# One hybrid decoder layer on one core: a written-out TensorE order for the norm stage, with two feed-forward products placed around the last tile's transposes

## The chip, the cores and the metric

The kernel runs on one core of one Trainium2 chip. The metric is the device time of one execution in microseconds (us), as the median of several runs; lower is better. A profile of one execution stands beside it.

## The reference

One layer of a decoder trunk, on 1024 tokens of width 1024, all in float32. Only the second half of the layer is touched by the change:

```python
mixed = jnp.concatenate([out_a..., out_b...], axis=-1)     # outputs of the two attention groups
x = x + ga1 * (mixed @ w_out[l])                           # 1024 -> 1024
h2 = rmsnorm(x, g_ffn[l]) * (1.0 + sc2) + sh2
gate, up = jnp.split(h2 @ w_gu[l], 2, axis=-1)             # 1024 -> 2 x 2816
x = x + ga2 * ((jax.nn.silu(gate) * up) @ w_down[l])
return rmsnorm(x, g_final)
```

## The kernel before

The tokens lie in eight tiles of 128. Every float32 matrix product is made of three products of rounded parts (low by high, high by high, high by low), so each operand is split into a high part (a copy on ScalarE) and a low part (a subtraction on VectorE or GpSimd). The feed-forward products are further combined in Winograd's manner: the activations and the weights are quartered, and sums of quarters are multiplied.

The stage in question begins once attention is done. A first pass multiplies all tiles by the first half of w_out (lines 1126 to 1137). The second pass, called the norm stage here, runs over the tiles in the order 0, 4, 1, 5, 2, 6, 3, 7 (line 1099), in the loop of lines 1217 to 1222. For a tile, `normed` loads the second half of the mixed rows, splits them (line 1108 on ScalarE, line 1109 on GpSimd), makes 24 products with w_out (two column halves of 12, through `mm3`, lines 366 to 368), adds them to the residual (line 1173, VectorE), sums the squares (line 1176, ScalarE), stores the residual to DRAM from the GpSimd queue (line 1177), computes the reciprocal root in small steps (`rstd_parts`, lines 157 to 163) and writes the normalized rows into `xn` (line 1179, VectorE). There is one `xn`, so a tile's rows can be written only when its predecessor's have been transposed. `turned` transposes `xn` in eight blocks on TensorE (line 1186), four into a PSUM bank of the kind `tp`, four into one of the kind `o`, and brings them back with scale and shift (line 1190 on ScalarE, line 1193 on VectorE). `combined` forms the quarter sums and splits them (lines 1159 and 1160, and sums at 1202 and 1208 to 1214): a tile below 4 completes columns of the quarters `22` and `S1`; a tile from 4 on completes columns of `11`, `S3`, `S2`, `12` and `S4`, and needs its partner of the lower half. The last tile below 4 is tile 3, the seventh in order; the last of all is tile 7.

The feed-forward loop (line 1291) then takes 22 blocks of 128 columns of w_gu. For each, `ff_prep` loads four weight quarters over the SP queue into the buffers that the residual tiles held (`ff_w`, line 1247), makes sums of them (`t1` to `t4`), and splits seven operands (`page_split`, lines 1240 on ScalarE and 1241 on VectorE); `ff_mm` makes a product of 12 matmuls (lines 1256 to 1258). In the first block the product of `w1` with `S1` (called p5) and that of `w4` with `22` (called p4) are written ahead of the other five, of which the first is `w11` with the quarter `11`.

What sets the order: each engine works through its own queue in order. A scheduler orders the queues ahead of time from the order of the program, from priorities and from its estimate of when inputs are ready. It may therefore place products of later tiles ahead of a tile's transposes. `ahead(PF)` (lines 1225, 1251 and 1292) raises the priority of the first block's preparation by 100. `on_pe` (line 759) takes that freedom away for the TensorE instructions that go through it: each is queued behind the one before it. Before the change the attention uses it and the norm stage doesn't.

Of the kernel before, what the change touches and what calls it, by code (L numbers as in the profile page):

```python
# [19 lines left out]
D = 1024  # L20
S = 1024
P = 128
# [46 lines left out]
def hybrid_block(ctx, tc, x, c, w_ada, b_ada, g_attn, w_in, kv_norm_g, w_uk, w_uv, w_out, g_ffn,  # L69
                 w_gu, w_down, g_final, lnm, out, dbg=None):  # L70
    nc = tc.nc
    V, A, G, PE = nc.vector, nc.scalar, nc.gpsimd, nc.tensor
# [23 lines left out]
    def mm_tile(tag="mm"):  # L96
        return ps["pool"].tile([P, 512], F32, name=tag, tag=tag, bufs=ps[tag])
# [24 lines left out]
    ident = const.tile([P, P], F32, name="ident")  # L122
# [31 lines left out]
    def rstd_parts(ss, width):  # L154

        m = small.tile([P, 8], F32, name="rm", tag="rm")[:, :1]
        V.tensor_scalar(m, ss, 1.0 / width, EPS, op0=OP.mult, op1=OP.add)
        y = small.tile([P, 8], F32, name="ry", tag="ry")[:, :1]
        A.activation(y, m, AF.Sqrt)
        V.reciprocal(y, y)  # L160
        t = small.tile([P, 8], F32, name="rt", tag="rt")[:, :1]
        V.scalar_tensor_tensor(t, y, m, y, op0=OP.mult, op1=OP.mult)
        V.tensor_scalar(t, t, -0.5, 1.5, op0=OP.mult, op1=OP.add)
        return y, t
# [193 lines left out]

    mods = modulation()

    def mm3(p, lhs, rhs, ks):

        n = len(ks)
        for j, k in enumerate(ks):
            (ah, al), (bh, bl) = lhs(k), rhs(k)
            PE.matmul(p, al, bh, start=(j == 0), stop=False)  # L366
            PE.matmul(p, ah, bh, start=False, stop=False)  # L367
            PE.matmul(p, ah, bl, start=False, stop=(j == n - 1))  # L368

    def pair3(ps_, qh, ql, qs, kh, kl_, ks, mm=PE.matmul):  # L370

# [302 lines left out]
    while True:  # L674
        while made < due:
            with behind(signed[0]):
                ev, n = next(work)
# [81 lines left out]
    def on_pe(op, *args, **kw):  # L759

        with tc.issue_after(pe_last[0].ins) if pe_last[0] else nullcontext():
            pe_last[0] = op(*args, **kw)  # L762
# [266 lines left out]
    for t in range(NT):  # L1029
        p = mm_tile()  # L1030
# [63 lines left out]
    f6 = [wk.tile([P, 3, 512], F32, name=f"f6{i}") for i in range(2)]  # L1094
# [4 lines left out]
    order = [0, 4, 1, 5, 2, 6, 3, 7]  # L1099
# [3 lines left out]
    def mixed(g, t):  # L1103
# [5 lines left out]
        (G if g else V).tensor_tensor(ml, mr, mh.bitcast(F32), op=OP.subtract)  # L1109
        return mh, ml  # L1110

    def w_out_part(m, w, e):
        p = mm_tile()
        cs = slice(e * 512, e * 512 + 512)
        mm3(p, lambda k: (m[0][:, k], m[1][:, k]), lambda k: (w[0][:, k, cs], w[1][:, k, cs]), range(4))
        return p

    first = order[4:] + order[:4]
# [8 lines left out]
    for i, t in enumerate(first):  # L1127
        m = mixed(0, t)
        residual(i + 1)
        for e in range(2):  # L1130
            cs = slice(e * 512, e * 512 + 512)
# [11 lines left out]
    def quarters(at, names):  # L1143
        return {n: [at.tile([P, 4, 512], F32R, name=f"A{n}{x}") for x in "hl"] for n in names}

    qA = quarters(pool(qr_ctx, "qR"), ("11", "S2"))
    qA.update(quarters(pool(qa_ctx, "qS"), ("S1", "22", "12", "S3", "S4")))
    xn = f6[0][:, 0:2].rearrange("p a b -> p (a b)")
# [4 lines left out]
    def h32_tile():  # L1153
        nh32[0] += 1
        return h32s[(nh32[0] - 1) % len(h32s)]
# [6 lines left out]
    R2, R1, EV = "GVG", "VGGVVVGG", "AAVAAAVA"  # L1162
    hq = {}

    def normed(n, t):

        if n >= 4:
            acc[t] = slot[n - 4]
            nc.sync.dma_start(acc[t], spill_y[n - 4])
        m = mixed(1, t)  # L1170
        for e in range(2):
            cs = slice(e * 512, e * 512 + 512)
            V.tensor_tensor(acc[t][:, cs], acc[t][:, cs], w_out_part(m, wo1, e), op=OP.add)
        dump(("x1", t), acc[t])
        ss = small.tile([P, 8], F32, name="ss", tag="ss")[:, :1]
        A.activation(f2.bitcast(BF), acc[t], AF.Square, accum_out=ss)
        G.dma_start(spill_x[t], acc[t])
        y, u = rstd_parts(ss, D)
        V.tensor_scalar(xn, acc[t], u, y, op0=OP.mult, op1=OP.mult)

    def turned(t):
        hq[t] = [h32_tile().rearrange("p (a b) -> p a b", b=P) for _ in range(2)]
        for k0, hv in zip((0, 4), hq[t]):
            p = mm_tile(("tp", "o")[k0 // 4])
            for k in range(4):
                PE.transpose(p[:, k * P:(k + 1) * P], xn[:, (k0 + k) * P:(k0 + k + 1) * P], ident)
            for k in range(4):
                kk = k0 + k
                if EV[kk] == "A":
                    A.activation(hv[:, k], p[:, k * P:(k + 1) * P], AF.Identity,  # L1190
                                 scale=a2[:, kk:kk + 1], bias=s2[:, kk:kk + 1])
                else:
                    V.tensor_scalar(hv[:, k], p[:, k * P:(k + 1) * P], a2[:, kk:kk + 1], s2[:, kk:kk + 1],
                                    op0=OP.mult, op1=OP.add)

    def combined(t):

        sl = slice(t % 4 * P, t % 4 * P + P)
        ha, hb = hq[t]
        if t < 4:  # L1200
            e_ = [{'G': G, 'V': V}[x] for x in R2]
            e_[0].tensor_tensor(s_, ha, hb, op=OP.add)
            split("22", hb, sl, e_[1])
            split("S1", s_, sl, e_[2])
            return
        a21, a22 = hq[t - 4]
        e_ = [{'G': G, 'V': V}[x] for x in R1]
        e_[0].tensor_tensor(a21, ha, a21, op=OP.subtract)
        e_[1].tensor_tensor(a22, a22, a21, op=OP.subtract)
        split("11", ha, sl, e_[3])  # L1210
        split("S3", a21, sl, e_[4])
        split("S2", a22, sl, e_[5])
        split("12", hb, sl, e_[6])
        e_[2].tensor_tensor(hb, hb, a22, op=OP.subtract)
        split("S4", hb, sl, e_[7])

    for n, t in enumerate(order):
        normed(n, t)
        turned(t)
        if n:  # L1220
            combined(order[n - 1])
    combined(order[-1])


    PF, PD = 100, 50
# [11 lines left out]
    def page_split(src):  # L1237
        h_, l_ = (pages[(used[0] + i) % len(pages)] for i in range(2))
        used[0] += 2
        A.activation(h_, src, AF.Copy)  # L1240
        V.tensor_tensor(l_, src, h_.bitcast(F32), op=OP.subtract)  # L1241
        return h_, l_
# [7 lines left out]
    def ahead(n):  # L1250
        return tc.high_priority(n) if n else nullcontext()

    def ff_mm(w, a, tag):
        p = mm_tile(tag)
        for k in range(4):
            PE.matmul(p, w[1][:, k], a[0][:, k], start=(k == 0), stop=False)  # L1256
            PE.matmul(p, w[0][:, k], a[0][:, k], start=False, stop=False)  # L1257
            PE.matmul(p, w[0][:, k], a[1][:, k], start=False, stop=(k == 3))  # L1258
        return p

    def u_tile():
# [3 lines left out]
    def ff_prep(f):  # L1265
        b11, b21 = ff_w(f * P)
        b12, b22 = ff_w(DFF + f * P)
        t1, t2, t3, t4 = tsum
        if f == 0:
            V.tensor_tensor(t1, b12, b11, op=OP.subtract)  # L1270
            w1 = page_split(t1)
            V.tensor_tensor(t2, b22, t1, op=OP.subtract)
            G.tensor_tensor(t4, b21, t2, op=OP.subtract)
            w4 = page_split(t4)
            w11 = page_split(b11)
        else:
            w11 = page_split(b11)
            G.tensor_tensor(t1, b12, b11, op=OP.subtract)
            G.tensor_tensor(t2, b22, t1, op=OP.subtract)
        w2 = page_split(t2)  # L1280
        w21 = page_split(b21)
        G.tensor_tensor(t3, b22, b12, op=OP.subtract)
        w3 = page_split(t3)
        if f > 0:
            w1 = page_split(t1)
            G.tensor_tensor(t4, b21, t2, op=OP.subtract)
            w4 = page_split(t4)
        w22 = page_split(b22)
        return w11, w21, w1, w2, w3, w4, w22

    for f in range(NF):
        with ahead(PF if f == 0 else 0):
            w11, w21, w1, w2, w3, w4, w22 = ff_prep(f)
        x_, u2, u3, u5 = [u_tile() for _ in range(4)]
        if f == 0:
            p5, p4 = ff_mm(w1, qA["S1"], "tp"), ff_mm(w4, qA["22"], "o")
        A.activation(x_, ff_mm(w11, qA["11"], "mm"), AF.Copy)
        V.tensor_tensor(u2, ff_mm(w2, qA["S2"], "tp"), x_, op=OP.add)
        V.tensor_tensor(x_, ff_mm(w21, qA["12"], "mm"), x_, op=OP.add)
        A.activation(x_, x_, AF.Silu)  # L1300
        V.tensor_tensor(u3, ff_mm(w3, qA["S3"], "mm"), u2, op=OP.add)
        if f > 0:
            p5 = ff_mm(w1, qA["S1"], "tp")
        V.tensor_tensor(u5, p5, u3, op=OP.add)
        V.tensor_tensor(u2, p5, u2, op=OP.add)
        if f > 0:
            p4 = ff_mm(w4, qA["22"], "o")
        V.tensor_tensor(u3, p4, u3, op=OP.add)
        A.activation(u3, u3, AF.Silu)  # L1309
        G.tensor_tensor(u5, u3, u5, op=OP.mult)  # L1310
        G.dma_start(spill_g[f][:, :512], u5)
        V.tensor_tensor(u2, ff_mm(w22, qA["S4"], "mm"), u2, op=OP.add)
        G.tensor_tensor(u2, x_, u2, op=OP.mult)
        G.dma_start(spill_g[f][:, 512:], u2)
# [230 lines left out]
```

## Time and profile before

| what | value |
|---|---|
| median of 3 runs | 1441.33 us (1437.42 to 1443.82) |
| the profiled execution's own time | 1437.92 us |
| its span, from the first to the last instruction | 1436.1 us |
| mean granted TensorE clock | 0.961 |
| TensorE busy | 1297.0 us (90%) |
| VectorE busy | 1016.3 us (71%) |
| GpSimd busy | 674.9 us (47%) |
| ScalarE busy | 598.8 us (42%) |

The norm stage lies at about 664 to 740 us of the span; the loop of the feed-forward part follows up to about 1166 us. A row of a timeline has the start, the duration, the engine, the line and the operation with its operands; "x4" says that four were merged into the row; in brackets stands how long the engine had been idle before, and what ended that. Names in a row are those of buffers: `f` stands for several buffers of the working pool (`xn`, the residual tiles, the sums), `wo` for the w_out buffers that later hold weight splits, `AS1l` for the low part of the quarter sum S1. PE is TensorE, DVE VectorE, ACT ScalarE, POOL GpSimd, SP the queue that issues most loads.

### The profile page before, as it was taken

How to read it: one execution, taken by the hardware profiler on the slowest of the kernel's cores; microseconds unless marked ns; L12 is line 12 of the kernel's file. 1: busy time of each engine (PE TensorE's matmuls, PEld its weight loads, DVE VectorE, ACT ScalarE, POOL GpSimd, SP SyncE). 2: the span in 40 equal slices, each digit the busy share in tenths (PEclk: the TensorE clock that was granted, in tenths of full speed). 3: DMA queues.
4: the chain of work that ended last, by engine and by line, in shares of the span. 5: the costliest groups of instructions: out<-in, count | busy, mean ns of one | idle time of the engine just before them, and what ended most of it. 6: DMA issues, size and time to landing. Idle time of an engine off the chain costs nothing.

```text
span 1436.1 us, 20358 instructions
## 1 busy us (share of the span) xinstructions
PE 1297.0 (90%) x7477; PEld 1033.9 (72%) x7477; DVE 1016.3 (71%) x1754; ACT 598.8 (42%) x1217; POOL 674.9 (47%) x454
## 2 busy tenths in 40 slices
PE   2999898999878899999869999999999998888894
PEld 0566776798666677787748888888888886766773
DVE  4136899999887477644987545554545569999997
ACT  3435546461456565613763333333333223223334
POOL 1650311324330598122676444445544436487865
PEclk9999898999989999999979999999999999999997
DMA  9723124233311444273423222222223281404004
GB/s 240 238 75 117 30 67 125 91 101 95 126 52 54 147 142 119 76 227 114 161 79 98 89 88 81 66 88 81 81 88 96 87 322 46 154 23 154 0 1 118
DMA packets 133018, 152.11 MB, mean 106 GB/s; under 512 B 9715, under 2 KB 95540, under 8 KB 132918
## 3 DMA queue, kind: packets, MB, share of 16 engines
q1 hardware_dynamic: 122160, 129.56, 29.8%
q0 software_dynamic: 4672, 15.73, 2.9%
q10 hardware_dynamic: 6086, 5.52, 1.5%
q8 instruction: 59, 0.97, 0.3%
q14 instruction: 41, 0.34, 0.1%
HBM read 115.65 MB, written 34.60 MB: 105 GB/s over the span
## 4 chain that ended last, share of the span: by engine, by line
PE 49%; DVE 29%; POOL 8%; DMA 6%; issue 5%; ACT 3%; SPq 1%; DVEq 0%; ACTq 0%; POOLq 0%
DVE score L620 7%; PE mm L1258 6%; PE mm L1256 6%; PE mm L1257 6%; PE tp L1256 3%; PE tp L1258 3%; PE tp L1257 3%; PE mm L366 3%; PE mm L368 3%; PE mm L367 2%; PE o L762 2%; DVE yacc L1376 2%; PE mm L762 2%; PE tp L762 2%; DVE score L424 2%
## 5 line engine op out<-in xcount | busy, mean ns | idle before, releaser
L1240 ACT ACTIVATE wo<-f 128x512 fp32r<-128x512 f32 x124 | 78.0, 631 | 178.0 <-PE mm L1258 78.8
L1241 DVE TENSOR_TENSOR wo<-f,wo 128x512 fp32r<-128x512 f32 x124 | 102.7, 831 | 43.8 <-ACT wo L1240 41.9
L366 PE MATMUL mm<-hh,wl 128*128 128x512 f32 (+2 forms) x288 | 111.7, 389 | 0.0
L367 PE MATMUL mm<-hh,wh 128*128 128x512 f32 (+2 forms) x288 | 111.2, 387 | 0.0
L368 PE MATMUL mm<-hl,wh 128*128 128x512 f32 (+2 forms) x288 | 108.1, 385 | 0.0
L214 POOL TENSOR_SCALAR wh<-wraw 128x1024 fp32r<-128x1024 f32 (+1 forms) x20 | 20.3, 1032 | 132.6 <-PE mm L368 82.3
L366 PE MATMUL mm<-wo,wo 128*128 128x512 f32 x148 | 59.0, 398 | 10.1 <-DVE wo L1366 10.1
L215 POOL TENSOR_TENSOR wl<-wraw,wh 128x1024 fp32r<-128x1024 f32 (+1 forms) x22 | 52.6, 2410 | 29.8 <-ACT ry L144 29.7
L366 PEld LDWEIGHTS mm<-hh,wl 128*128 128x128 f32 (+1 forms) x288 | 54.4, 189 | 15.2 <-issue 2.8
L368 PEld LDWEIGHTS mm<-hl,wh 128*128 128x128 f32 (+1 forms) x288 | 53.7, 188 | 14.0 <-issue 2.2
L367 PEld LDWEIGHTS mm<-hh,wh 128*128 128x128 f32 (+1 forms) x288 | 54.6, 190 | 11.5 <-issue 1.1
L368 PE MATMUL mm<-wo,wo 128*128 128x512 f32 x148 | 56.9, 393 | 1.7 <-DVE wo L1366 1.7
L367 PE MATMUL mm<-wo,wo 128*128 128x512 f32 x148 | 58.2, 393 | 0.0
L793 ACT ACTIVATE ttB<-ttB,mn 128x128 f32<-128x128 f32 (+7 forms) x64 | 49.1, 768 | 15.5 <-DVE mn L789 14.9
L1366 DVE TENSOR_TENSOR wo<-f,wo 128x1536 fp32r<-128x1536 f32 (+1 forms) x17 | 55.1, 3246 | 0.0
L1310 POOL TENSOR_TENSOR f<-f 128x512 f32<-128x512 f32 x15 | 19.8, 1322 | 74.2 <-ACT f L1309 74.2
L366 PE MATMUL mm<-wo,ml 128*128 128x512 f32 x128 | 51.6, 403 | 1.8 <-DVE ml L1109 1.8
L762 PE MATMUL tp<-ident,ttB 128*128 128x128 f32 x288 | 43.6, 294 | 10.2 <-ACT ptB L808 9.7
L620 DVE TENSOR_SCALAR_CACHE_REDUCE score<-kl,sc 128x1024 bf16<-128x1024 uint16 (+2 forms) x48 | 52.3, 1140 | 0.0
L620 DVE TENSOR_SCALAR_CACHE_REDUCE score<-ka,sc 128x768 bf16<-128x768 int16 (+2 forms) x48 | 52.3, 1139 | 0.0
L367 PE MATMUL mm<-wo,mh 128*128 128x512 f32 x128 | 51.0, 398 | 0.0
L368 PE MATMUL mm<-wo,mh 128*128 128x512 f32 x128 | 50.9, 398 | 0.0
(469 smaller groups left out, 4238.7 us busy)
## 6 DMA issues: line engine op xcount, KB each, us to landing
f<-in_w_gu_dram SPq DMA_DIRECT2D x44, 512.0 KB, 3.8
spg<-f POOLq DMA_DIRECT2D x44, 256.0 KB, 2.8
wraw<-in_w_in_dram SPq DMA_DIRECT2D x21, 512.0 KB, 4.0
f<-spg SPq DMA_DIRECT2D x33, 256.0 KB, 3.0
va<-in_w_ada_dram SPq DMA_DIRECT2D x16, 512.0 KB, 4.2
wlm<-in_w_ada_dram SPq DMA_DIRECT2D x32, 256.0 KB, 2.7
f<-in_w_down_dram SPq DMA_DIRECT2D x23, 256.0 KB, 3.1
more<-in_w_down_dram SPq DMA_DIRECT2D x21, 256.0 KB, 5.4
```

Source lines behind the costliest of these rows:

```text
L215: G.tensor_tensor(lo, raw, hi.bitcast(F32), op=OP.subtract)
L366: PE.matmul(p, al, bh, start=(j == 0), stop=False)
L367: PE.matmul(p, ah, bh, start=False, stop=False)
L368: PE.matmul(p, ah, bl, start=False, stop=(j == n - 1))
L620: V.tensor_scalar(mask(t, u), keys[:, seg[t]], z[:, i:i + 1], 0.0, op0=OP.is_lt, op1=OP.add, accum_out=cnt[:, i:i + 1])
L762: pe_last[0] = op(*args, **kw)
L1240: A.activation(h_, src, AF.Copy)
L1241: V.tensor_tensor(l_, src, h_.bitcast(F32), op=OP.subtract)
L1256: PE.matmul(p, w[1][:, k], a[0][:, k], start=(k == 0), stop=False)
L1257: PE.matmul(p, w[0][:, k], a[0][:, k], start=False, stop=False)
L1258: PE.matmul(p, w[0][:, k], a[1][:, k], start=False, stop=(k == 3))
L1366: V.tensor_tensor(l_, x, h_.bitcast(F32), op=OP.subtract)
```

## The change

The loop's body is reordered: `normed` is parted into `added` (load, split, products, residual, squares, store, small steps) and `normed` (the line that writes `xn`). For each tile after the first, `added` of the tile comes first, then `turned` of its predecessor, then `normed` of the tile, then `combined` of the predecessor. The products and the transposes of the norm stage go through `on_pe`, so that TensorE keeps this order. The last tile's `turned` and `combined` move into the first `ff_prep`: p5 goes through `on_pe` behind the transposes of tile 3, then come the transposes of tile 7, then p4, then `combined` of tile 7. `t4` of the first block gets another buffer.

```diff
--- before.py
+++ after.py
@@ -358,14 +358,14 @@
 
     mods = modulation()
 
-    def mm3(p, lhs, rhs, ks):
+    def mm3(p, lhs, rhs, ks, mm=PE.matmul):
 
         n = len(ks)
         for j, k in enumerate(ks):
             (ah, al), (bh, bl) = lhs(k), rhs(k)
-            PE.matmul(p, al, bh, start=(j == 0), stop=False)
-            PE.matmul(p, ah, bh, start=False, stop=False)
-            PE.matmul(p, ah, bl, start=False, stop=(j == n - 1))
+            mm(p, al, bh, start=(j == 0), stop=False)
+            mm(p, ah, bh, start=False, stop=False)
+            mm(p, ah, bl, start=False, stop=(j == n - 1))
 
     def pair3(ps_, qh, ql, qs, kh, kl_, ks, mm=PE.matmul):
 
@@ -1109,10 +1109,13 @@
         (G if g else V).tensor_tensor(ml, mr, mh.bitcast(F32), op=OP.subtract)
         return mh, ml
 
+    def fixed(*a, **kw):
+        on_pe(PE.matmul, *a, **kw)
+
     def w_out_part(m, w, e):
         p = mm_tile()
         cs = slice(e * 512, e * 512 + 512)
-        mm3(p, lambda k: (m[0][:, k], m[1][:, k]), lambda k: (w[0][:, k, cs], w[1][:, k, cs]), range(4))
+        mm3(p, lambda k: (m[0][:, k], m[1][:, k]), lambda k: (w[0][:, k, cs], w[1][:, k, cs]), range(4), fixed)
         return p
 
     first = order[4:] + order[:4]
@@ -1162,7 +1165,7 @@
     R2, R1, EV = "GVG", "VGGVVVGG", "AAVAAAVA"
     hq = {}
 
-    def normed(n, t):
+    def added(n, t):
 
         if n >= 4:
             acc[t] = slot[n - 4]
@@ -1175,7 +1178,9 @@
         ss = small.tile([P, 8], F32, name="ss", tag="ss")[:, :1]
         A.activation(f2.bitcast(BF), acc[t], AF.Square, accum_out=ss)
         G.dma_start(spill_x[t], acc[t])
-        y, u = rstd_parts(ss, D)
+        return rstd_parts(ss, D)
+
+    def normed(t, y, u):
         V.tensor_scalar(xn, acc[t], u, y, op0=OP.mult, op1=OP.mult)
 
     def turned(t):
@@ -1183,7 +1188,7 @@
         for k0, hv in zip((0, 4), hq[t]):
             p = mm_tile(("tp", "o")[k0 // 4])
             for k in range(4):
-                PE.transpose(p[:, k * P:(k + 1) * P], xn[:, (k0 + k) * P:(k0 + k + 1) * P], ident)
+                on_pe(PE.transpose, p[:, k * P:(k + 1) * P], xn[:, (k0 + k) * P:(k0 + k + 1) * P], ident)
             for k in range(4):
                 kk = k0 + k
                 if EV[kk] == "A":
@@ -1215,11 +1220,12 @@
         split("S4", hb, sl, e_[7])
 
     for n, t in enumerate(order):
-        normed(n, t)
-        turned(t)
+        yu = added(n, t)
+        if n:
+            turned(order[n - 1])
+        normed(t, *yu)
         if n:
             combined(order[n - 1])
-    combined(order[-1])
 
 
     PF, PD = 100, 50
@@ -1250,12 +1256,12 @@
     def ahead(n):
         return tc.high_priority(n) if n else nullcontext()
 
-    def ff_mm(w, a, tag):
+    def ff_mm(w, a, tag, mm=PE.matmul):
         p = mm_tile(tag)
         for k in range(4):
-            PE.matmul(p, w[1][:, k], a[0][:, k], start=(k == 0), stop=False)
-            PE.matmul(p, w[0][:, k], a[0][:, k], start=False, stop=False)
-            PE.matmul(p, w[0][:, k], a[1][:, k], start=False, stop=(k == 3))
+            mm(p, w[1][:, k], a[0][:, k], start=(k == 0), stop=False)
+            mm(p, w[0][:, k], a[0][:, k], start=False, stop=False)
+            mm(p, w[0][:, k], a[1][:, k], start=False, stop=(k == 3))
         return p
 
     def u_tile():
@@ -1267,12 +1273,14 @@
         b12, b22 = ff_w(DFF + f * P)
         t1, t2, t3, t4 = tsum
         if f == 0:
+            t4 = f6[1][:, 2].rearrange("p (k c) -> p k c", c=P)
             V.tensor_tensor(t1, b12, b11, op=OP.subtract)
             w1 = page_split(t1)
             V.tensor_tensor(t2, b22, t1, op=OP.subtract)
             G.tensor_tensor(t4, b21, t2, op=OP.subtract)
             w4 = page_split(t4)
             w11 = page_split(b11)
+            early_mm(w1, w4)
         else:
             w11 = page_split(b11)
             G.tensor_tensor(t1, b12, b11, op=OP.subtract)
@@ -1288,12 +1296,21 @@
         w22 = page_split(b22)
         return w11, w21, w1, w2, w3, w4, w22
 
+    p54 = []
+
+    def early_mm(w1, w4):
+
+        p54.append(ff_mm(w1, qA["S1"], "tp", fixed))
+        turned(order[-1])
+        p54.append(ff_mm(w4, qA["22"], "o", fixed))
+        combined(order[-1])
+
     for f in range(NF):
         with ahead(PF if f == 0 else 0):
             w11, w21, w1, w2, w3, w4, w22 = ff_prep(f)
         x_, u2, u3, u5 = [u_tile() for _ in range(4)]
         if f == 0:
-            p5, p4 = ff_mm(w1, qA["S1"], "tp"), ff_mm(w4, qA["22"], "o")
+            p5, p4 = p54
         A.activation(x_, ff_mm(w11, qA["11"], "mm"), AF.Copy)
         V.tensor_tensor(u2, ff_mm(w2, qA["S2"], "tp"), x_, op=OP.add)
         V.tensor_tensor(x_, ff_mm(w21, qA["12"], "mm"), x_, op=OP.add)
```

## Rows read from the trace of the kernel before

**Rows 1.** Four stretches: length; PE, PEld, DVE, ACT, POOL busy; TensorE clock; DMA share, GB/s.

```profile
664.00:680.00 16.00, 16.00 (x74) 13.01 (x73) 6.25 (x16) 6.52 (x12) 5.09 (x5) 1.00 0.34 114
680.00:715.30 35.30, 34.13 (x167) 27.48 (x165) 32.09 (x51) 25.37 (x59) 22.77 (x20) 1.00 0.46 154
715.30:740.40 25.10, 9.79 (x32) 6.92 (x31) 25.03 (x36) 19.38 (x45) 17.81 (x14) 0.59 0.33 99
740.40:780.00 39.60, 39.60 (x171) 32.07 (x172) 31.07 (x33) 16.25 (x28) 31.97 (x24) 1.00 0.35 105
```

**Rows 2.** TensorE's waits from 664 to 741: in total, times, longest.

```profile
PE tp L1186 <- DVE f L1179: 12.9, 2, 7.2
PE mm L1258 <- DVE A11l L1160: 1.1, 1, 1.1
```

**Rows 3.** Timeline of TensorE in the norm stage.

```profile
663.75 0.40 PE L366 MATMUL mm<-wo,ml 128*128 128x512 f32 x1
...
678.44 0.40 PE L366 MATMUL mm<-wo,ml 128*128 128x512 f32 x1
678.67 0.60 PE L1186 MATMUL tp<-ident,f 128*128 128x128 f32 x4
...
679.47 0.47 PE L367 MATMUL mm<-wo,mh 128*128 128x512 f32 x1
...
715.05 0.40 PE L368 MATMUL mm<-wo,mh 128*128 128x512 f32 x1
722.64 1.09 PE L1186 MATMUL tp<-ident,f 128*128 128x128 f32 x4 [7.19 <-DVE f L1179]
723.52 1.06 PE L1186 MATMUL o<-ident,f 128*128 128x128 f32 x4
730.32 1.08 PE L1186 MATMUL tp<-ident,f 128*128 128x128 f32 x4 [5.74 <-DVE f L1179]
731.19 1.06 PE L1186 MATMUL o<-ident,f 128*128 128x128 f32 x4
732.82 0.80 PE L1256 MATMUL tp<-AS1h,wo 128*128 128x512 f32 x1 [0.56 <-ACT AS1h L1159]
...
740.38 0.50 PE L1258 MATMUL mm<-A11l,wo 128*128 128x512 f32 x1 [1.15 <-DVE A11l L1160]
```

**Rows 4.** Timeline of VectorE in the norm stage.

```profile
674.07 0.81 DVE L1179 TENSOR_SCALAR f<-f,rt,ry 128x1024 f32<-128x1024 f32 x1
...
700.59 4.18 DVE L162 SCALAR_TENSOR_TENSOR rt<-ry,rm 128x1 f32<-128x1 f32 x1
...
715.80 3.10 DVE L1241 TENSOR_TENSOR wo<-f,wo 128x512 fp32r<-128x512 f32 x2
...
721.65 0.84 DVE L1179 TENSOR_SCALAR f<-f,rt,ry 128x1024 f32<-128x1024 f32 x1
...
733.45 1.76 DVE L1160 TENSOR_TENSOR A22l<-f,A22h 128x512 fp32r<-128x512 f32 x1
...
735.46 0.67 DVE L1272 TENSOR_TENSOR f<-f,f 128x512 f32<-128x512 f32 x1
...
737.96 0.68 DVE L1241 TENSOR_TENSOR wo<-f,wo 128x512 fp32r<-128x512 f32 x1
```

**Rows 5.** Timeline of GpSimd: low part of S1, first and last tile, and `t4`.

```profile
684.95 1.27 POOL L1160 TENSOR_TENSOR AS1l<-f,AS1h 128x512 fp32r<-128x512 f32 x1
...
732.94 1.71 POOL L1160 TENSOR_TENSOR AS1l<-f,AS1h 128x512 fp32r<-128x512 f32 x1
...
745.11 1.62 POOL L1273 TENSOR_TENSOR f<-f,f 128x512 f32<-128x512 f32 x1
```

**Rows 6.** Timeline of TensorE in the first w_out pass, behind a short wait.

```profile
651.12 0.50 PE L366 MATMUL mm<-wo,ml 128*128 128x512 f32 x1 [1.84 <-DVE ml L1109]
...
653.06 0.63 PE L367 MATMUL mm<-wo,mh 128*128 128x512 f32 x1
653.49 0.63 PE L368 MATMUL mm<-wo,mh 128*128 128x512 f32 x1
```

## The prediction

> **What bounds the kernel now.** I first looked at the busy times by stretch. From 664 to 715.3 us TensorE is hardly ever idle (16.00 of 16.00, 34.13 of 35.30), and behind 740.4 it is never idle (39.60 of 39.60). Between lies a hole: of 25.10 us TensorE is busy for 9.79, at a mean granted clock of 0.59, while VectorE is busy for 25.03 [rows 1]. The reader is to see two things: what the change can win lies in this hole, and the engine that is full in it is VectorE, not TensorE.
>
> The waits of TensorE come next. 12.9 us of the hole are two waits for the line that writes `xn`, and 1.1 us is a wait for the low part of the quarter 11 [rows 2]. The timeline of TensorE shows why. The scheduler let the products of w_out run ahead: the last starts at 715.05, but the transposes of the seventh tile (tile 3) start at 722.64 and those of the eighth (tile 7) at 730.32. p5 starts at 732.82, and the first product of the feed-forward part then stands still until 740.38 [rows 3]. From there TensorE runs without a gap, so whatever lets that product finish earlier, or takes products out of what follows it, shortens the kernel one for one.
>
> **The change, part by part.** All durations are those of the profiled execution. It took 1437.92 us (its span of 1436.1 and 1.8 outside); the median of the three runs, 1441.33, is 3.4 above that. I work out a difference and take it from the median.
>
> *Order of the products (reorders, adds nothing).* From 663.75 to 678.44 lie 63 starts of products, so 0.233 us for one and 5.6 for the 24 of a tile; eight transposes take 679.47 - 678.67 = 0.8 [rows 3]. In the new order the transposes of the k-th tile (k from 0) can't start ahead of 663.75 + 5.6 (k + 2) + 0.8 k. For the first that is 674.95, and its `xn` is written at 674.07 + 0.81 = 674.88 [rows 4], so it starts 3.7 us earlier than now. For the seventh it is 713.35, against 722.64.
>
> *The seventh tile's transposes.* The early bound is 713.35. The late one keeps VectorE's pace and gains only the 3.7 at the start: 718.9. A gain of nothing is excluded, since VectorE was busy for only 6.25 of the first 16.00 us [rows 1]. VectorE's fullness speaks for the late end; for the early end speaks that two weight subtractions of 3.10 us stood ahead of this `xn` [rows 4], and that the second half of the first block's preparation now ranks behind the last tile's work. I take the middle, 716.1, and 1.4 for the transposes (0.8 at the full rate, 1.96 as measured now, 723.52 + 1.06 - 722.64): done at 717.5.
>
> *S1.* From the end of the transposes to the end of the low part of S1 it takes 684.95 + 1.27 - 679.47 = 6.8 us with the first tile, where little else was queued, and 732.94 + 1.71 - 724.58 = 10.1 with the seventh [rows 3, 5]. I take the middle, 8.4: S1 is complete at 725.9. `t4` (1.62 us on GpSimd [rows 5]) may now stand in front of it; that goes into the late bound. Its new buffer frees it from waiting for the last tile, and otherwise costs nothing: w4 is wanted only behind the last tile's transposes, and without that cover it would add its 1.62 and a split.
>
> *p5 ahead of the last tile's transposes.* This is an added wait: in TensorE's queue the last transposes, p4 and all else now stand behind S1. p5 is 12 products: 2.8 us at 0.233, or 5.1 at the 0.43 between products at the lower rate [rows 6]. TensorE will have been idle for some 8 us, and p5 started at the lower rate now too, so I take 4.6: done at 730.5. The last transposes take 0.8 to 1.96; I take 1.2: done at 731.7. Now they are done at 731.19 + 1.06 = 732.25 [rows 3].
>
> *From there to the first product of 11.* Now 740.38 - 732.25 = 8.1 us. Three pieces on VectorE in it are no part of what 11 needs and are either forced ahead (the low part of 22, 1.76, and t2, 0.67) or ranked behind (a weight subtraction, 0.68): 3.1 together [rows 4]. That leaves 5.0 to 8.1; as the first two can't stay where they are, I take 5.2: 736.9. Now two of its 12 products are done ahead of 740.38, so that corresponds to 739.9: 3.0 us earlier.
>
> *p4.* Its 12 products leave the gapless part and stand in the hole: 2.8 us off. *The clock.* Between p4's end (734.5) and 736.9 TensorE waits 2.4 us. After a wait of 1.84 us some products went at 0.43 [rows 6]. For the product of 11 that is 0 to 12 x 0.2 = 2.4 us; I take 0.5, as a busy stretch of 4 us (p5's end, transposes, p4) lies ahead of it. The Trainium skill, "TensorE: Matmul & The Clock Gate", section on oscillation, warns that bursts of products between waits are throttled again at each wait; by it the whole product would go at the lower rate and the forecast would be 1.9 us later, 1437.9. The clock of 0.59 in the hole agrees with that so far.
>
> *Queues passed.* `added` issues its loads on SP and its store on GpSimd ahead of the predecessor's transposes now; they were issued in that order of tiles before too, and each waits for what it waited for. I cost them at nothing: the products, 5.6 us a tile, cover a load; uncovered, a load would be late by what a TensorE wait shows.
>
> **Sum:** 3.0 + 2.8 - 0.5 = 5.3 us; 1441.33 - 5.3 = 1436.0. All early ends together: transposes done at 714.15, S1 at 720.9, p5 at 723.7, transposes at 724.5, 11 at 729.5, so 10.4 + 2.8 = 13.2 less, 1428.1. All late ends: 720.9, with t4 732.6, 737.7, 739.6, 747.8, so 7.9 later, 2.8 back and 2.4 for the clock, 7.5 more: 1448.8.
>
> **The rivals.**
>
> *A, the products set the pace.* VectorE keeps up, `xn` of the seventh tile is ready at 713, and S1 comes in under 7 us: 1428 to 1432, say 1430. For it: the first tile's chain, and VectorE's idle start. Against it: 32.09 of 35.30 busy [rows 1], and stalls such as a small step of 4.18 us [rows 4], which nothing in the change removes. 0.20.
>
> *B, the last transposes are held up by S1 (slower).* In TensorE's queue they stand behind p5, p5 behind the low part of S1 on GpSimd. Now S1 ends at 734.65, 2.4 us after those transposes are done. With my other terms the gain is used up when S1 ends 5.3 us later than 725.9, at 731.2; at the late bound, 732.6 with the slower rate and the old 8.1 behind, it is 1448.8. For it: GpSimd alone decides, and S1 took 10.1 us. Against it: the start is 3.7 us earlier. The Trainium skill, "PSUM — Partial Sum Buffer", section on engine and sequencer instructions, says that matmuls start and complete in program order, so nothing could overtake p5; no row here shows an overtaking. 0.11.
>
> *C, the gain is taken back in the feed-forward part.* It starts earlier, but its weights don't come earlier: VectorE and GpSimd are busy for 31.07 and 31.97 of the 39.60 us behind 740.4 [rows 1], and the last tile's sums stand in the same queues as the splits of the other five products. New waits of 4 us in the first block give 1440. 0.18. That the change doesn't reach the order is hardly possible, as a link between TensorE instructions is binding.
>
> **How the numbers follow.** The forecast, 1432 to 1440, has 0.51. A measurement of this kernel can't tell less than about 0.5%, 7.2 us, from no change. Faster by over 7.2 (below 1434.1): all of A, and 0.15 of the forecast: 0.35. Slower by over 7.2 (above 1448.5): only B towards its end and beyond, with what is unforeseen: 0.10. Same: 0.55. The range 1428.5 to 1443.5 leaves out the far end of A and most of B; the forecast's own is 1432 to 1440.
>
> **What would show it.** Right: the seventh tile's transposes at 714 to 719, p5 starting at 724 to 728 on a wait for S1, the last transposes right behind it, p4 directly after them and then a short wait for the low part of 11 until about 737. In the hole, TensorE's waits for `xn` give way to a wait for S1. Wrong: waits for `xn` at most tiles with products ending well behind 716; p5 waiting for w1; p4 waiting for w4; a new idle time of TensorE in the first feed-forward block.

## The result and the profile after

The changed kernel takes 1450.88 us (median of four runs, 1450.65 to 1453.40), the kernel before 1439.88 (four runs, 1437.42 to 1443.82): 1.0076 times as long, 95% interval 1.0052 to 1.0100. The forecast was 1436.0, the upper end of its range 1443.5. The profiled execution took 1450.65 us, with a span of 1448.9 and a mean granted clock of 0.957; in it TensorE is busy for 1303.9 us, VectorE for 1012.4, GpSimd for 679.9 and ScalarE for 599.6. The work is the same. Of the 12.7 us between the two spans, 6.9 are TensorE's busy time, in which a product at the lower rate counts longer, and 5.8 its idle time.

What lies ahead of the norm stage keeps its instruction order on every queue, but its duration varies: the stage's first product starts anywhere from 660.7 to 674.5 us over the profiled executions of this study. So marks are counted from that first product below (663.75 before [rows 3], 666.68 after), and the **stage length** is the time from it to the start of the last feed-forward product. Two executions of the changed kernel (the second is experiment 8) agree within 0.5 us at the starts of the transposes, of p5 and of 11, and within 1.0 us in the stage length; p4's start differs by 1.2. The stage length is 501.4 us before and 511.1 after: all but 3.0 us of the difference between the spans, and 2.9 of these lie ahead of the stage.

The first four lines are the stretches of [rows 1] in the trace after, the last one the second stretch counted from the stage's start, as [rows 1] has it (length; PE, PEld, DVE, ACT, POOL busy; clock; DMA share, GB/s):

```profile
664.00:680.00 16.00, 16.00 (x75) 12.94 (x74) 5.87 (x12) 5.78 (x10) 4.42 (x4) 1.00 0.25 82
680.00:715.30 35.30, 27.99 (x125) 22.69 (x124) 26.15 (x45) 24.22 (x56) 23.67 (x21) 0.92 0.43 148
715.30:740.40 25.10, 14.50 (x64) 11.45 (x63) 21.23 (x35) 16.34 (x38) 13.59 (x11) 0.77 0.36 118
740.40:780.00 39.60, 34.83 (x138) 27.52 (x139) 31.28 (x35) 18.33 (x33) 30.15 (x22) 0.87 0.32 93
...
682.93:718.23 35.30, 27.99 (x124) 22.59 (x123) 27.32 (x48) 23.61 (x53) 23.36 (x20) 0.90 0.43 148
```

The reader is to see the last line: in the stretch where before both engines were nearly full (34.13 and 32.09 of 35.30), TensorE now does 27.99 and VectorE 27.32. No engine is the bound there; they wait for each other. TensorE's waits from 655 to 1182 us, as [rows 2], say the same from its side:

```profile
PE tp L762 <- DVE f L1184: 14.1, 4, 6.8
PE tp L762 <- ACT AS1h L1162: 5.2, 1, 5.2
PE mm L1262 <- ACT A11h L1162: 2.1, 1, 2.1
```

The timeline of TensorE, as [rows 3], with the first transposes of each tile, then p5, the last tile's transposes, p4 and the first product of 11:

```profile
677.88 0.65 PE L762 MATMUL tp<-ident,f 128*128 128x128 f32 x4
686.13 0.66 PE L762 MATMUL tp<-ident,f 128*128 128x128 f32 x4 [1.57 <-DVE f L1184]
695.99 1.09 PE L762 MATMUL tp<-ident,f 128*128 128x128 f32 x4 [3.17 <-DVE f L1184]
704.06 0.60 PE L762 MATMUL tp<-ident,f 128*128 128x128 f32 x4
713.27 1.08 PE L762 MATMUL tp<-ident,f 128*128 128x128 f32 x4 [2.57 <-DVE f L1184]
721.25 0.60 PE L762 MATMUL tp<-ident,f 128*128 128x128 f32 x4
734.62 1.09 PE L762 MATMUL tp<-ident,f 128*128 128x128 f32 x4 [6.76 <-DVE f L1184]
735.50 1.06 PE L762 MATMUL o<-ident,f 128*128 128x128 f32 x4
741.72 1.22 PE L762 MATMUL tp<-AS1h,wo 128*128 128x512 f32 x2 [5.16 <-ACT AS1h L1162]
...
748.01 0.60 PE L762 MATMUL tp<-ident,f 128*128 128x128 f32 x4
748.45 0.60 PE L762 MATMUL o<-ident,f 128*128 128x128 f32 x4
748.80 0.71 PE L762 MATMUL o<-A22h,wo 128*128 128x512 f32 x2
...
753.94 0.78 PE L1262 MATMUL mm<-A11h,wo 128*128 128x512 f32 x1 [2.11 <-ACT A11h L1162]
```

From the stage's start the eight transposes begin at 11.2, 19.4, 29.3, 37.4, 46.6, 54.6, 67.9 and 81.3 us; before at 14.9, 21.2, 27.4, 35.7, 42.2, 49.7, 58.9 and 66.6. The 3.7 us won at the first tile are lost by the third, which is 1.9 late; the delay then grows to 4.4 at the fifth, 9.0 at the seventh and 14.8 at the last. VectorE's queue ahead of the seventh tile's `xn` shows what it stands behind (its line has number 1184 now, 1179 in [rows 4]):

```profile
725.10 0.69 DVE L1176 TENSOR_TENSOR f<-f,mm 128x512 f32<-128x512 f32 x1 [0.23 <-PE mm L762]
725.70 0.69 DVE L1213 TENSOR_TENSOR f<-f,f 128x512 f32<-128x512 f32 x1
726.31 0.16 DVE L160 RECIPROCAL ry<-ry 128x1 f32<-128x1 f32 x1
726.38 0.68 DVE L1247 TENSOR_TENSOR wo<-f,wo 128x512 fp32r<-128x512 f32 x1
726.97 1.25 DVE L162 SCALAR_TENSOR_TENSOR rt<-ry,rm 128x1 f32<-128x1 f32 x1
728.14 2.35 DVE L1247 TENSOR_TENSOR wo<-f,wo 128x512 fp32r<-128x512 f32 x2
730.41 0.14 DVE L163 TENSOR_SCALAR rt<-rt 128x1 f32<-128x1 f32 x1
730.48 0.68 DVE L1163 TENSOR_TENSOR A11l<-f,A11h 128x512 fp32r<-128x512 f32 x1
731.07 0.67 DVE L1176 TENSOR_TENSOR f<-f,mm 128x512 f32<-128x512 f32 x1
731.67 0.68 DVE L1163 TENSOR_TENSOR AS3l<-f,AS3h 128x512 fp32r<-128x512 f32 x1
732.27 2.20 DVE L1184 TENSOR_SCALAR f<-f,rt,ry 128x1024 f32<-128x1024 f32 x1
```

Line 1176 is the residual addition, and both here belong to the **next** tile: the first of them could not run before 725.06, because its products stand in TensorE's queue behind the sixth tile's transposes of 721.25. Three weight splits (line 1247), a sum and two of the predecessor's low parts stand there too. TensorE has done the next tile's products meanwhile and waits the 6.76 us.

### The profile page after: what moved, and what is told of

Its sections match the earlier page's. It is cut to its first block, busy times and chain, and to the rows that moved or that the text cites. A ratio compares the mean times of both kernels' runs of the same rounds, so it can differ in the third digit from the quotient of the medians.

```text
span 1448.9 us, 20361 instructions
## 1 busy us (share of the span) xinstructions
PE 1303.9 (90%) x7477; PEld 1039.3 (72%) x7477; DVE 1012.4 (70%) x1754; ACT 599.6 (41%) x1217; POOL 679.9 (47%) x454
## 4 chain that ended last, share of the span: by engine, by line
PE 51%; DVE 28%; POOL 7%; DMA 6%; issue 4%; ACT 2%; SPq 1%; DVEq 0%; ACTq 0%; POOLq 0%
DVE score L620 7%; PE mm L1262 6%; PE mm L1263 6%; PE mm L1264 6%; PE mm L762 5%; PE tp L1262 3%; PE tp L1264 3%; PE tp L1263 3%; PE o L762 3%; PE mm L366 2%; DVE wo L1383 2%; PE mm L368 2%; PE mm L367 2%; DVE yacc L1393 2%; PE tp L762 2%
## 5 line engine op out<-in xcount | busy, mean ns | idle before, releaser
L1246 ACT ACTIVATE wo<-f 128x512 fp32r<-128x512 f32 x124 | 78.1, 632 | 178.3 <-PE mm L1264 80.9
L762 PE MATMUL mm<-wo,mh 128*128 128x512 f32 x256 | 80.5, 396 | 0.0
L762 PEld LDWEIGHTS mm<-wo,mh 128*128 128x128 f32 x256 | 48.9, 191 | 10.9 <-issue 0.2
L793 ACT ACTIVATE ttB<-ttB,mn 128x128 f32<-128x128 f32 (+7 forms) x64 | 49.1, 768 | 16.2 <-DVE mn L789 15.6
```

## The experiments

Two theories stood at first. **Order** (T in the expectations): the written order leaves the products a lead of one tile, which means that only the next tile's products are done when a tile's transposes start, so that TensorE and VectorE wait for each other tile by tile. **Hold** (U in the expectations; rival B): p5, fixed ahead of the last tile's transposes, holds them up. Times below are medians beside that of the kernel before in the same job; ratios, worked out from all runs and not the quotient of the medians, have their 95% interval; marks and stage lengths are of the profiled execution.

**1. The feed-forward part alone**: the norm stage's products are free again.

```diff
-        mm3(p, lambda k: (m[0][:, k], m[1][:, k]), lambda k: (w[0][:, k, cs], w[1][:, k, cs]), range(4), fixed)
+        mm3(p, lambda k: (m[0][:, k], m[1][:, k]), lambda k: (w[0][:, k, cs], w[1][:, k, cs]), range(4))
```

> The changed kernel, but the products of w_out may again run ahead of the transposes; the feed-forward part of the change stays. Theory T (the fixed order is the cost: a tile's products now stand behind its predecessor's transposes, and VectorE's queue has the row of xn behind additions that need those products): as before or faster, 1433 to 1440, with the transposes of the seventh tile about 59 us behind the first product, as before. Theory U (the cost is p5 in TensorE's queue ahead of the last tile's transposes): 1446 to 1451, as the changed kernel.

1441.51 against 1441.19, ratio 1.0015 [0.9988, 1.0042]; stage 502.9. The time lies in neither range, but as before, which T allowed. The eight transposes begin as before, but for the last, and so do all `xn`, to 0.1 us. TensorE's timeline from the seventh tile's transposes on:

```profile
723.90 1.09 PE L762 MATMUL tp<-ident,f 128*128 128x128 f32 x4 [7.21 <-DVE f L1184]
...
735.08 1.22 PE L762 MATMUL tp<-AS1h,wo 128*128 128x512 f32 x2 [9.24 <-ACT AS1h L1162]
...
741.31 1.05 PE L762 MATMUL tp<-ident,f 128*128 128x128 f32 x4
...
745.54 0.40 PE L1262 MATMUL mm<-A11h,wo 128*128 128x512 f32 x1
```

The hold is real: the last `xn` is written at 66.5 and transposed at 76.4, and 11 starts 5.8 us later than before. Against that, 11 waited for another 1.15 us within its product before, and p4's 2.8 us are out of the gapless part, so that the stage is only 1.5 longer.

**2. The fixed order alone**: the feed-forward part is as before.

```diff
+    turned(order[-1])
+    combined(order[-1])
...
-            early_mm(w1, w4)
...
-            p5, p4 = p54
+            p5, p4 = ff_mm(w1, qA["S1"], "tp"), ff_mm(w4, qA["22"], "o")
```

> The fixed order of products and transposes alone; both feed-forward products and the last tile's part stay where they were before. T: 1449 to 1455, the same waits for xn at the transposes as the changed kernel (14 us together), the seventh tile's transposes about 68 us behind the first product. U: 1438 to 1444, since p5 no longer holds the last transposes.

1447.83, ratio 1.0033 [1.0009, 1.0056]; stage 507.7. The time lies between the two ranges; the seventh tile's transposes start at 68.0, as T has it, and the `xn` waits are all there:

```profile
PE tp L762 <- DVE f L1184: 21.4, 5, 7.3
```

So of the 9.75 us of the stage the fixed order costs 6.27 by itself; the feed-forward part costs 1.47 by itself and 3.47 on top of the order.

**3. Fixed, but with a lead of two tiles**: is it that the order is fixed, or which order?

```diff
     for n, t in enumerate(order):
-        yu = added(n, t)
+        pend[n] = added(n, t)
+        if n >= 2:
+            turned(order[n - 2])
         if n:
-            turned(order[n - 1])
-        normed(t, *yu)
-        if n:
-            combined(order[n - 1])
+            normed(order[n - 1], *pend[n - 1])
+        if n >= 2:
+            combined(order[n - 2])
+    turned(order[6])
+    normed(order[7], *pend[7])
+    combined(order[6])
```

> The changed kernel with another fixed order: the transposes of a tile come behind the products of the next two tiles instead of one. T: the products have a lead again, the waits for xn fall below 8 us, 1436 to 1443. Rival V (VectorE's own work makes xn late, whatever the lead of the products): 1448 to 1453, xn as late as in the changed kernel.

1444.13 against 1441.19, 1.1 above T's range and 3.9 below V's, ratio 1.0017 [0.9993, 1.0042]; stage 503.1, 8.0 below the change's. The stretch that answers to the last line of the windows above:

```profile
681.79:717.09 35.30, 33.99 (x171) 27.78 (x170) 31.81 (x55) 28.29 (x65) 25.32 (x21) 1.00 0.54 171
```

Both engines are full again, under an order that is written out just as firmly. The last `xn` is even written at 61.8, 4.6 us ahead of before. That is not turned into time, as TensorE's waits show:

```profile
PE tp L762 <- DVE wo L1252: 10.4, 1, 10.4
PE tp L762 <- DVE f L1184: 6.8, 1, 6.8
PE tp L762 <- POOL AS1l L1163: 1.5, 1, 1.5
```

p5 now waits 10.4 us for the low part of `w1`, which VectorE writes, and the last transposes stand behind p5, until 76.5.

**4. One tile's lead, with the next tile's additions queued behind `xn`** on VectorE:

```diff
-            V.tensor_tensor(acc[t][:, cs], acc[t][:, cs], w_out_part(m, wo1, e), op=OP.add)
+            p = w_out_part(m, wo1, e)
+            with tc.issue_after(xl[0].ins) if xl[0] else nullcontext():
+                V.tensor_tensor(acc[t][:, cs], acc[t][:, cs], p, op=OP.add)
```

> The changed kernel, but in VectorE's queue the additions of the next tile's products are put behind the line that writes xn. T, in its form that the ring of waits (xn behind additions, additions behind products, products behind the predecessor's transposes) is the cost: 8 us of waits vanish, 1440 to 1445. If only the lost lead counts and not the queue on VectorE: 1448 to 1453.

1448.94, ratio 1.0039 [1.0013, 1.0064]: the median misses the range of the ring and lies in that of the lost lead alone, and the ratio is not told from the change's. In the trace the stage is 507.6, 3.6 less than the change's. `xn` of the second to sixth tile is written at 17.4, 26.0, 34.2, 42.4 and 50.3, where the change has 19.4, 29.2, 36.7, 46.4 and 53.1. But the seventh comes at 63.7, against 58.7 before and 67.8 in the change: three weight splits and the sum `t1` still stand ahead of it. So by the marks the additions are a part of the cost; the times do not show it.

**5. The last tile's transposes ahead of p5**, with free products (first) and with the change's order (second):

```diff
-        p54.append(ff_mm(w1, qA["S1"], "tp", fixed))
         turned(order[-1])
+        p54.append(ff_mm(w1, qA["S1"], "tp", fixed))
```

> Products of w_out free to run ahead, and the last tile's transposes ahead of p5 instead of behind it; p4 and t4 as in the change. The earlier run with free products showed the last transposes held up 9.2 us behind p5 and its wait for S1, with no net gain. If that hold is what eats p4's 2.8 us: 1437 to 1440 where the kernel before has 1441, last transposes at about 67 us behind the first product as before. If the tail is set by VectorE's queue anyhow: 1440 to 1443.

> The changed kernel with the last tile's transposes ahead of p5. If p5 ahead of them is what the change pays on top of the fixed order alone (that run was at 1447.8, the changed kernel at 1450.9): 1445 to 1448. If not: 1449 to 1452.

With free products 1445.55 against 1441.89, ratio 1.0023 [1.0008, 1.0039]; stage 503.0. The hoped-for gain is missing, and the median is above both ranges: every mark up to the start of 11 is within 0.6 us of before, and the products of 11, which are free, pass p4 in TensorE's queue, so that nothing fills the hole. With the change's order 1451.51, ratio 1.0056 [1.0038, 1.0074]; stage 509.7, only 1.5 below the change's. (Its seventh transposes, which the edit does not touch, start at 69.0, 1.1 later than the change's; counted from them the gain is 2.6.) TensorE waits for `xn` instead of for S1:

```profile
PE tp L762 <- DVE f L1184: 22.4, 5, 8.3
```

This refutes the hold as the main cause: taken away, most of the loss stays.

**6. The splits of `w21` and `w22` of the first block, and of `w11`, `w21` and `w22` of the second, queued on ScalarE and VectorE behind the last tile's sums**, in the kernel before (first) and in the change (second):

```diff
-        A.activation(h_, src, AF.Copy)
-        V.tensor_tensor(l_, src, h_.bitcast(F32), op=OP.subtract)
+        with tc.issue_after(last["A"].ins) if held else nullcontext():
+            A.activation(h_, src, AF.Copy)
+        with tc.issue_after(last["V"].ins) if held else nullcontext():
+            V.tensor_tensor(l_, src, h_.bitcast(F32), op=OP.subtract)
...
-        w21 = page_split(b21)
+        w21 = page_split(b21, f < 2)
```

> The kernel before, with one edit: the weight splits that the first feed-forward products don't need (w21 and w22 of block 0, w11, w21, w22 of block 1) are queued behind the last tile's sums on ScalarE and VectorE. Theory V2 (VectorE's queue, with weight splits in front of the rows of the last two tiles, sets the hole): 3 to 6 us faster than before, 1435 to 1438, xn of the seventh tile 2 to 4 us earlier. Rival (VectorE's waits are for S1, evacuations and loads, and the splits fill idle time or only move): within 2 us of 1441, or slower by a new wait for w21 in block 0.

> The changed kernel with the same edit. V2: the wait of 6.8 us ahead of the seventh tile's transposes falls to 3 or 4, and the whole to 1445 to 1448. If that wait is the ring through products and additions: 1449 to 1452.

In the kernel before, S1 ends at 69.0 instead of 70.9 and 11 starts at 71.7 instead of 74.9: what stands in VectorE's and ScalarE's queues does set those two. But the seventh `xn` is only 1.1 us earlier, and the time is 1444.08 against 1441.89, far from V2's range, ratio 1.0016 [0.9998, 1.0033], stage 502.9: a new wait for the low part of `w2` takes the gain back.

```profile
PE tp L1260 <- DVE wo L1245: 4.1, 1, 4.1
```

In the change: 1450.89, in the range of the ring, ratio 1.0066 [1.0042, 1.0090], stage 509.8. The wait ahead of the seventh transposes falls from 6.8 to 4.5. The seventh `xn` is 2.1 us and the last 4.5 us earlier, of which 1.4 reach the end. So by the stage the splits are a smaller part than the additions.

**7. Two tiles' lead with the transposes first** (edits 3 and 5; first), **and the second block's splits held as well** (edit 6 for that block alone; second). Can the earlier rows be turned into time?

> Products two tiles ahead in a fixed order, and the last tile's transposes ahead of p5. With the lead of two, xn of the last tile was ready 61.8 us behind the first product, where the kernel before has 66.4, and its transposes waited until 76.5 for p5. Theory L (the lead of the products decides, and p5 hides it): last transposes at 62, the first product of 11 at 70 to 72 (before: 74.9), 1437 to 1440 against 1441, and 9 to 12 us below the run with one tile's lead and the same tail. Rival (the tail is VectorE's and gives it back): 11 at 75 or later, 1441 to 1444.

> The same, with the weight splits of block 1 queued behind the last tile's sums. If VectorE's queue in the tail is what is left: the first product of 11 another 1 to 3 us earlier, 1435 to 1439. If a later split is then late, as w2 was in the run with five splits held: no gain on the run without it.

The first: 1442.24 against 1440.69, ratio 1.0013 [0.9998, 1.0028]; stage 502.6, 7.1 below that of experiment 5 with the same tail (9 to 12 were expected). The marks are L's, the time is the rival's. The last transposes start at 61.9, 4.7 ahead of before, and 11 starts at 71.6, but among p5's products, which waited for `w1`:

```profile
736.13 1.19 PE L762 MATMUL tp<-AS1h,wo 128*128 128x512 f32 x2 [6.80 <-DVE wo L1252]
737.12 0.63 PE L1267 MATMUL mm<-A11h,wo 128*128 128x512 f32 x1
```

The second: 1438.88, ratio 0.9991 [0.9975, 1.0007]; stage 501.3, the same as before. The time is in the expected range, but 11 starts at 75.5, no earlier. It is the best of the set, and no faster than the kernel before.

**8. The change once more**, beside the same runs of the kernel before, to see how well its marks repeat:

> The changed kernel once more, beside the two others on the same chip: 1449 to 1452, with the marks within the stage (xn, transposes, p5, 11, counted from the first product) within 0.5 us of the first trace, if the differences between runs of one kernel lie ahead of the stage.

1448.47 against 1440.69, ratio 1.0051 [1.0037, 1.0066]; stage 510.2, and 11 at 86.8. The marks named lie within 0.5 us of the first trace; p4 starts 1.2 us later. The interval lies clear of those of experiment 7, which ran beside it: with a lead of two tiles the times show no loss that is clear of the noise.

**9. One tile's lead with VectorE's queue cleared**: edits 4, 5 and 6 together (6 moves ScalarE's copies too). What stood open was whether the short lead costs because of what is queued ahead of `xn` on VectorE, or because the products themselves leave the chain no slack.

> One tile's lead as in the change, with VectorE's queue mended in both places: additions behind the line that writes xn, and five weight splits behind the last tile's sums; the last tile's transposes ahead of p5. Theory Q (the short lead hurts only by what stands ahead of xn in VectorE's queue): xn of the seventh tile at 58 to 61 us behind the first product (before 58.7, change 67.8), the stage within 504 us (before 501.3, change 511.1), 1439 to 1443. Theory L (a lead of one tile is too short by itself): xn of the seventh at 63 or later, the stage at 507 or more, 1446 to 1450.

1445.56 against 1442.02, ratio 1.0018 [1.0002, 1.0035]; stage 504.4. The seventh `xn` is written at 60.9, where the change has 67.8; a split and the sum `t1`, 1.69 and 1.74 us, stand right ahead of it still:

```profile
719.10 1.74 DVE L1284 TENSOR_TENSOR f<-f 128x512 f32<-128x512 f32 x1
720.77 0.80 DVE L1189 TENSOR_SCALAR f<-f,rt,ry 128x1024 f32<-128x1024 f32 x1
```

The mark of `xn` is that of the queue theory (Q) and the stage 0.4 above its range; the median lies between the two ranges, nearer to L's, and the profiled execution is the fastest of the twelve. By the marks 6.9 of the 9.0 us at the seventh `xn`, which edit 5 doesn't touch, and 6.8 of the 9.7 of the stage come back with the lead left at one tile. So most of the cost is what stands queued ahead of `xn` (edit 5 by itself gave back 1.5). ScalarE's share was not tried apart; in the change's trace it did not hold up the seventh `xn`, since its root of that tile is done at 725.38 and VectorE comes to the reciprocal at 726.31. The 3.0 that stay are not divided further.

## Why the prediction was wrong

The sum went wrong in the main in one step. From the stage's start:

**Order of the products.** Right for the first tile: its transposes start at 11.2, as worked out from 674.95.

**The seventh tile's transposes: the step that failed.** Forecast 716.1, or 52.4 from the start, with 55.2 as the late end; measured 67.9, 15.6 us late and 9.0 later than before. The late end "keeps VectorE's pace" and carries the first tile's 3.7 us on to the seventh; a gain of nothing was excluded because VectorE was idle for much of the first 16 us. But pace belongs to the order: before, 2.7 tiles' products have started when the first transposes do (the 63 starts of the prediction's own count) and 6.9 at the fifth, a lead of 1.6 to 1.9 tiles, and VectorE has additions to do while a tile's other steps are under way. With one tile's lead the additions come late, stand in VectorE's queue with splits and low parts ahead of `xn`, and TensorE, which may do no further products, waits for it. The 9.0 us can be followed on VectorE: the seventh tile's second addition, which follows its products, starts 4.7 later than before, counted from the stage's start (first line before, second after), another 3.0 are lost between it and the start of `xn`, and `xn` itself takes 1.4 longer.

```profile
713.83 0.67 DVE L1173 TENSOR_TENSOR f<-f,mm 128x512 f32<-128x512 f32 x1
...
721.44 0.69 DVE L1176 TENSOR_TENSOR f<-f,mm 128x512 f32<-128x512 f32 x1
```

The argument for the early end, that weight splits would rank behind this `xn` now, failed as well: three stand ahead of it, as many as before. Experiment 3 (the lead restored: 8.0 us back) and experiment 9 (the queue cleared: 6.8 back) show it from two sides. The prediction named the sign to look for ("waits for `xn` at most tiles with products ending well behind 716") and gave it no chance of its own.

**The chain behind it** held. The transposes took 736.56 - 734.62 = 1.9 us (forecast 1.4, from a 1.96 that by its own rows is 1.94); S1 was complete 7.7 later (8.4), `t4` right ahead of its low part:

```profile
740.76 1.79 POOL L1280 TENSOR_TENSOR f<-f,f 128x512 f32<-128x512 f32 x1
742.52 1.71 POOL L1163 TENSOR_TENSOR AS1l<-f,AS1h 128x512 fp32r<-128x512 f32 x1
```

p5 was done 3.8 later (4.6), the last transposes took 0.8 (1.2), and 11 started 5.1 behind them (5.2). Together 19.3, forecast 20.8.

**p4 and the clock.** p4 stands in the hole, as forecast. 11 cost more: of its 12 products the first eight ran at a granted clock of 0.51, the 1.2 GHz level, behind the wait of 2.11 us; 753.94 to 758.40 is 4.5 us, 1.7 over the full rate, where 0.5 was taken and 2.4 was the bound. The Trainium skill, "TensorE: Matmul & The Clock Gate", section on oscillation, warns of bursts of products that start slowly again behind waits; this trace agrees for the first eight products. That the whole product would go slowly was the prediction's own reading. In the second execution (experiment 8) the wait was 0.26 us, the granted clock 1.00, and the 12 products took 3.2 us: this term differs from execution to execution.

**The account.** 11 starts at 87.3, forecast 73.1 (736.9): 14.1 late. With 1.2 more for the clock and the 5.3 of the forecast gain, 10.0 us slower; the stage is 9.7 longer.

*Queues passed*, costed at nothing, held: no product of w_out waits in the stage.

**Rival A** was wrong: the seventh `xn` was to be ready at 713, or 49.3, and came at 67.8. **Rival B** was right about the mechanism: the last transposes start at 81.3, though their `xn` is written at 78.1, and in experiment 1 at 76.4 instead of 66.5. The Trainium skill, "PSUM — Partial Sum Buffer", on engine and sequencer instructions (matmuls start in program order), agrees with those two rows. But it was not the main cost: the whole feed-forward part costs 1.5 us alone and 3.5 on top of the order, and undoing the hold in the change gives 1.5 back. S1 ended at 77.5, beyond the point from which B decides (731.2, or 67.5), because the rows came late. **Rival C** fell: from 740.38 before and from 753.94 here to its last blocks, the feed-forward loop has no gap on TensorE, 424.92 of 424.92 us before and now

```profile
753.94:1178.00 424.06, 424.06 (x1824) 344.68 (x1825) 227.47 (x304) 139.18 (x220) 210.76 (x177) 1.00 0.29 91
```

Waits of the kind that C priced at 4 us, for weight splits, do appear in experiments 3, 6 and 7 (10.4, 4.1 and 6.8 us), where rows or S1 come earlier than before. That they are why no order tried here beats the kernel before is argued, not shown: holding splits back (experiment 7, second) brought the stage to the length before and no further.

## What to carry to other kernels

An order written out for one engine also fixes how far it may run ahead of the others; before fixing it, read from the trace how many tiles it runs ahead now, and write an order that keeps this lead. Follow the row that the moved work waits for in the **other** engine's queue, and cost everything that will stand ahead of it there, not only the waits of the engine that is reordered. Where executions differ by more than the effect, compare marks inside the changed stage, counted from its own start.

## What was not expected of the hardware

The line of `xn` (128x1024 on VectorE) takes 0.81 us in two tiles of the changed kernel and 1.06 to 2.20 in the other six; the slow ones coincide with an instruction of GpSimd. Beside the 2.20 us at 732.27 GpSimd has

```profile
732.64 1.27 POOL L1219 TENSOR_TENSOR f<-f,f 128x512 f32<-128x512 f32 x1
```

and 0.81 + 1.27 = 2.08. The Trainium skill, "SBUF — State Buffer", section "Who interferes with whom", says that the two engines share a pair of ports as an exclusive lock, so that the later one is blocked until the other's instruction is done. The length of this row agrees with it; its start doesn't, as VectorE's row begins 0.37 us ahead of GpSimd's and is the one that is stretched (a DMA issue on GpSimd, 732.04 to 732.61, lies just ahead). The small step of 4.18 us [rows 4] doesn't fit one instruction: three of GpSimd, of 1.3 us each, lie beside it. What decides between one and three was not tried.

Executions of one kernel differ by up to 14 us (experiment 4, 1442.31 to 1456.70; the kernel before, 1436.93 to 1448.91 in one job), while in the profiled ones the marks of the norm stage mostly repeat to a few tenths where the order is the same (experiment 5 has an exception of 1.1 us), and the stage's start moves. The cause of that was not looked for.
